# Receptance and key of the RWKV heads: two matmuls per k-tile in place of three

## The chip, the cores and the metric

The kernel runs on one core of one Trainium2 chip. Its time is the device time of one execution in microseconds; the number used for a kernel is the median of its runs. A lower time is better.

## The reference

A two-layer decoder trunk on 256 tokens of width 2048, in float32. Layer 0 mixes tokens with a short gated convolution, layer 1 with RWKV-7 time mixing; each is followed by a feed-forward part with a short convolution inside. All the change lies in layer 1, in two of its projections:

```python
xx = jnp.pad(x, ((0, 0), (1, 0), (0, 0)))[:, :-1] - x
xm = x[None] + xx[None] * mu[:, None, None, :]
xr, xw, xk, xv, xa, xg = xm[0], xm[1], xm[2], xm[3], xm[4], xm[5]
r = xr @ w_r
k = xk @ w_k
v = xv @ w_v
```

`r` is the receptance and `k` the key, each a 256 x 2048 by 2048 x 2048 product. They are then cut into 32 heads of 64 channels, and a recurrence over the tokens runs in every head.

## The kernel before

Precision: TensorE multiplies in a reduced float32 form, so each operand is kept as a high and a low part (`hl`, index 0 and 1), and a product is the sum of three matmuls: high by high, high by low, low by high. `mm3` (L144 to L147) issues these three. A weight arrives from memory as `raw` (1 MB, three buffers), and `split_w` makes its parts in pieces of 1024 columns: ScalarE writes the high part (L136), VectorE the low one (L137), into four rotating buffers `hl`.

Layer 0 and the ffn's up-projections use another form, `column` (L191 to L202): the activations' high and low part lie side by side for each k-tile, so one matmul of 512 columns gives high by high and high by low in the two halves of a PSUM bank, and a second one of 256 columns adds low by high to the second half. `column_sum` (L204 to L207) then copies one half out with ScalarE and adds the other with VectorE.

The heads: 16 pairs of heads are worked through in a software pipeline of four stages, written as Python generators (`rwkv_heads`, from L577). In one step, stage 3 of one pair, stage 2 of the next, stage 1 of the one after it and stage 0 of the newest take turns: each is advanced to its next `yield`, in the order 3, 2, 1, 0, until all are done. Stage 0 (L591) makes two small projections (`tw`, `ta`) and then receptance and key for 128 channels, 16 k-tiles each, from `wr[g]` and `wk[g]`, by `group_a`, which issues `mm3` 16 times on 256 columns and yields after every fourth k-tile. Both sums share one PSUM bank (tag "big", two buffers), key in the first half and receptance in the second; one ScalarE copy (L606) takes both out into `kr`. Stage 1 makes the chunk's decay and key terms from `kr` (a square at L635 that TensorE sums at L641, products at L666 and L670) and small matmuls of 64 x 64 blocks. Stage 2 inverts a 64 x 64 triangular matrix by levels (TensorE L724 and L734, VectorE L726, ScalarE L736, and a last step at L741 to L756). Stage 3 runs the recurrence over four chunks (L763 to L792) and the output's norm and gate.

Order: the code gives a priority; the framework's planner, which estimates when each instruction could start, writes the order of every engine's queue, so an instruction may be moved ahead of older ones that are not ready. TensorE's order in the trace shows this: a single matmul of a group of `mm3` can stand between pieces of other stages.

The activations: the shifted mixtures are made by `variant` (L484) for receptance (`xr`, L478), key (`xk`, in four tiles of `Early.tile`, L417) and the small projections (`lora`, L500). In the old layout a tile has the index order token block, k-tile, part, token: the high parts of the two token blocks of one k-tile lie apart, and an operand of 256 columns is two blocks of 128. The value projection reads the same tiles in blocks of 128 tokens, as weights (L438).

Of the kernel before, what the change touches and what calls it, by code (L numbers as in the profile page):

```python
# [11 lines left out]
F32 = mybir.dt.float32  # L12
F32R = mybir.dt.float32r
F16 = mybir.dt.float16
AF = mybir.ActivationFunctionType
ALU = mybir.AluOpType
# [65 lines left out]
def trunk(ctx: ExitStack, tc: tile.TileContext, x, ng, vec, cst, gnp, win, wout, up0, dn0, wl1, wv, wr, wk, wl2, wo,  # L82
# [108 lines left out]
    def column(src, xhl):  # L191


        ps = bank8(2, T)
        kt = 0
        for hl in load_w(src, 1024 if KT >= 8 else KT * P):
            for i in range(min(8, KT)):
                W = slice(i * P, (i + 1) * P)
                nc.tensor.matmul(ps, hl[:, 0, W], xhl[:, kt], start=kt == 0, stop=False)  # L199
                nc.tensor.matmul(ps[:, 1], hl[:, 1, W], xhl[:, kt, 0], start=False, stop=kt == KT - 1)  # L200
                kt += 1
        return ps[:, 0], ps[:, 1]  # L202

# [203 lines left out]
    class Early:  # L407
# [9 lines left out]
        def tile(self, q):  # L417
            t = self.pool.tile([P, NB, 4, 2, P], F32R, name=f"xkv{q}")
            return t, t.rearrange("p b k h c -> p (b k h c)").rearrange("p (h c) -> p h c", h=2)
# [14 lines left out]
        def mm(self, ps, hls, r, blk):  # L434
            for i in range(2 * len(hls)):
                kt = int(r * (RAWW // 512)) + i
                hl, c, xm = hls[i // 2], i % 2 * 512, self.xv[kt // 4]
                mm3(ps[blk], xm[:, blk, kt % 4, 0, :], xm[:, blk, kt % 4, 1, :], hl[:, 0, c:c + 512],  # L438
                    hl[:, 1, c:c + 512], kt == 0, kt == KT - 1)
# [7 lines left out]
        def mix(self, n):  # L447
# [7 lines left out]
            split(self.xv[n][:, 0, :, 0, :], self.xv[n][:, 0, :, 1, :], xm)  # L455
# [17 lines left out]
    def rwkv(xT, lhid, ctxv, early):  # L473
# [4 lines left out]
        xr = ctxv.enter_context(sbuf("rvr", 1, "right")).tile([P, NB, KT, 2, P], F32R, name="xr")  # L478
        xv = early.xv

        with tc.tile_pool(name="rvar", bufs=2, reuse_waits="tile") as vp:
            xx = vp.tile([P, NB, KT, P], F32, name="xx", bufs=1)

            def variant(m, k4, dst, blks=slice(0, NB), nk=4, whole=False):  # L484
                xm = vp.tile([P, NB, 4, P], F32, name="xm", bufs=3)[:, :, :nk]
                for i in range(nk):
                    kt = k4 + i
                    mu = vcol("mu", m * KT + kt)
                    if whole:
                        nc.vector.scalar_tensor_tensor(xm[:, blks, i], xx[:, blks, kt], mu, xT[:, blks, kt, 1:P + 1],  # L490
                                                       ALU.mult, ALU.add)
                    else:
                        nc.scalar.activation(xm[:, blks, i], xx[:, blks, kt], AF.Copy, scale=mu)
                if not whole:
                    nc.vector.tensor_tensor(out=xm[:, blks], in0=xm[:, blks], in1=xT[:, blks, k4:k4 + nk, 1:P + 1], op=ALU.add)
                split(dst[:, blks, :, 0, :], dst[:, blks, :, 1, :], xm[:, blks])
# [3 lines left out]
            def lora(which, ms):  # L500
                ps = [bank8(512) for _ in range(2)]
                kt = 0
                for r in range(KT * GC // RAWW):
                    for hl in load_w(wl1[which][:, r * RAWW:(r + 1) * RAWW], 1024):
                        for i in range(4):
                            if i % 2 == 0:
# [3 lines left out]
                                for m in dict.fromkeys(ms):  # L510
                                    vts[m] = xl[:, len(vts) * 1024:(len(vts) + 1) * 1024].rearrange(
                                        "p (b k h c) -> p b k h c", b=NB, k=2, h=2)
                                    variant(m, kt, vts[m], nk=2)
                            for j in range(2):
# [3 lines left out]
                                    vt[:, :, i % 2, 0, :], vt[:, :, i % 2, 1, :], kt == 0, kt == KT - 1)  # L518
# [32 lines left out]
            def variants():  # L551
                for k4 in range(0, KT, 4):
                    variant(0, k4, xr[:, :, k4:k4 + 4])
                    yield
# [22 lines left out]
    def rwkv_heads(scr, xk, xr, lhid, ctxv, fill):  # L577
# [4 lines left out]
        with tc.tile_pool(name="kz", bufs=1, reuse_waits="tile") as zp, tc.tile_pool(name="kx", bufs=2, reuse_waits="tile") as kx, \  # L582
# [8 lines left out]
            def stage0(g, st):  # L591
# [4 lines left out]
                for w, dst in ((0, st.tw), (1, st.ta)):  # L596
# [4 lines left out]
                ps = bank("big", 2, T)  # L601
                yield from group_a(wr[g], xsel(xr), ps[:, 1], 0)
                yield from group_a(wk[g], lambda kt, j: (xk[kt // 4][:, :, kt % 4, 0, :], xk[kt // 4][:, :, kt % 4, 1, :]),
                                   ps[:, 0], 0)
                st.kr = kx.tile([P, 2, T], F32, name="kr")
                nc.scalar.activation(st.kr, ps, AF.Copy)  # L606
# [539 lines left out]
```

## Time and profile before

| | us |
|---|---|
| median of 3 runs | 2588.75 |
| lowest and highest run | 2586.83 and 2589.52 |
| the profiled execution | 2590.17 |
| its span | 2588.4 |
| stage of the heads, by the first and last start of the copy L606 | 1269.2 to 1701.6 |

In the profile, PE is TensorE, PEld its weight loads, DVE is VectorE, ACT is ScalarE, POOL is GpSimd and SP the queue that issues most transfers. L145 is line 145 of the kernel. A row in order of time has the start in us, the duration in us, engine, line, operation, output and inputs by the program's names, their shape, a count, and in brackets how long the engine was idle before and what ended that. Matmuls are pipelined: the duration of one includes its way through the array, and the next one starts earlier.

### The profile page before, as it was taken

What the parts mean: (1) busy time and instruction counts of PE and PEld (TensorE: products, weight loads), DVE (VectorE), ACT (ScalarE), POOL (GpSimd) and SP (SyncE); (2) the same over time, 40 slices, a digit from 0 to 9 for tenths busy, and PEclk for the clock granted to TensorE, in tenths of its full rate; (3) what the DMA queues carried; (4) which work ended last, traced back from release to release, by engine and by line L of the source; (5) the groups of instructions that cost most, each with busy time, mean ns of one, the idle gap of its engine ahead of it and who ended that gap; (6) DMA issues with size and microseconds to landing.
All of it is one profiled execution on the core that took longest, in us unless ns stands there. A gap on an engine that the chain in (4) does not pass through costs nothing.

```text
span 2588.4 us, 44203 instructions
## 1 busy us (share of the span) xinstructions
PE 2545.5 (98%) x18284; PEld 2192.6 (85%) x18284; DVE 1689.0 (65%) x2419; ACT 1351.7 (52%) x2115; POOL 166.3 (6%) x239
## 2 busy tenths in 40 slices
PE   7999999999999999989999999999999999999998
PEld 7888888888888888878888888877888888888886
DVE  5666567777767655589756666665767767765555
ACT  5444456555555544469744444443655555554444
POOL 0000000000000000010222223220000000000000
PEclk9999999999999999999999999999999999999999
DMA  6555554555555555545523222335455555555553
GB/s 229 189 196 185 191 194 157 187 194 189 186 195 190 186 194 185 205 165 204 179 83 105 95 92 92 103 112 212 163 196 186 188 195 186 188 195 194 194 190 138
DMA packets 106986, 446.89 MB, mean 173 GB/s; under 512 B 29760, under 2 KB 47824, under 8 KB 57248
## 3 DMA queue, kind: packets, MB, share of 16 engines
q1 hardware_dynamic: 105328, 437.40, 48.6%
q0 software_dynamic: 1456, 6.66, 0.7%
q8 instruction: 143, 2.34, 0.4%
q14 instruction: 59, 0.48, 0.1%
HBM read 436.03 MB, written 8.00 MB: 172 GB/s over the span
## 4 chain that ended last, share of the span: by engine, by line
PE 93%; DVE 2%; ACT 2%; POOL 1%; issue 1%; DMA 1%; SPq 0%; DVEq 0%; POOLq 0%; ACTq 0%
PE tl L199 8%; PE big L199 8%; PE mn L199 8%; PE inv L199 8%; PE big L145 5%; PE big L146 5%; PE big L147 5%; PE tl L200 4%; PE big L200 4%; PE inv L200 4%; PE mn L200 4%; PE tl L145 3%; PE tl L147 3%; PE mn L145 3%; PE mn L147 3%; PE mn L146 2%
## 5 line engine op out<-in xcount | busy, mean ns | idle before, releaser
L137 DVE TENSOR_TENSOR hl<-raw,hl 128x1024 fp32r<-128x1024 f32 (+1 forms) x818 | 975.3, 1195 | 498.1 <-ACT hl L136 493.9
L136 ACT ACTIVATE hl<-raw 128x1024 fp32r<-128x1024 f32 (+1 forms) x818 | 841.8, 1031 | 568.4 <-PE big L147 150.8
L199 PE MATMUL tl<-xhl,hl 128*128 128x512 f32 x880 | 307.8, 391 | 0.0
L199 PE MATMUL big<-xhl,hl 128*128 128x512 f32 x880 | 307.8, 391 | 0.0
L199 PE MATMUL mn<-xhl,hl 128*128 128x512 f32 x864 | 302.2, 391 | 0.0
L199 PE MATMUL inv<-xhl,hl 128*128 128x512 f32 x864 | 301.9, 391 | 0.0
L200 PE MATMUL tl<-xhl,hl 128*128 128x256 f32 x880 | 246.2, 280 | 0.0
L200 PE MATMUL big<-xhl,hl 128*128 128x256 f32 x880 | 246.2, 280 | 0.0
L200 PE MATMUL mn<-xhl,hl 128*128 128x256 f32 x864 | 241.8, 280 | 0.0
L200 PE MATMUL inv<-xhl,hl 128*128 128x256 f32 x864 | 241.7, 280 | 0.0
L199 PEld LDWEIGHTS big<-xhl,hl 128*128 128x128 f32 x880 | 165.0, 187 | 36.2
L199 PEld LDWEIGHTS tl<-xhl,hl 128*128 128x128 f32 x880 | 165.0, 187 | 36.2
L199 PEld LDWEIGHTS inv<-xhl,hl 128*128 128x128 f32 x864 | 161.9, 187 | 35.7
L199 PEld LDWEIGHTS mn<-xhl,hl 128*128 128x128 f32 x864 | 161.9, 187 | 35.5
L200 PEld LDWEIGHTS tl<-xhl,hl 128*128 128x128 f32 x880 | 165.6, 188 | 0.0
L200 PEld LDWEIGHTS big<-xhl,hl 128*128 128x128 f32 x880 | 165.6, 188 | 0.0
L200 PEld LDWEIGHTS inv<-xhl,hl 128*128 128x128 f32 x864 | 162.6, 188 | 0.0
L200 PEld LDWEIGHTS mn<-xhl,hl 128*128 128x128 f32 x864 | 162.6, 188 | 0.0
L308 POOL TENSOR_TENSOR r<-s,nhalf 128x1 f32<-128x1 f32 x16 | 9.7, 606 | 1243.3 <-DVE s L306 1243.3
L145 PE MATMUL big<-xr,hl 128*128 128x256 f32 x268 | 82.8, 309 | 0.0
L145 PE MATMUL big<-xkv,hl 128*128 128x256 f32 x256 | 77.9, 304 | 0.0
L146 PE MATMUL big<-xr,hl 128*128 128x256 f32 x268 | 77.1, 288 | 0.0
(514 smaller groups left out, 4989.1 us busy)
## 6 DMA issues: line engine op xcount, KB each, us to landing
raw<-in_up_dram SPq DMA_DIRECT2D x172, 1024.0 KB, 4.8
raw<-in_dn_dram SPq DMA_DIRECT2D x88, 1024.0 KB, 4.8
raw<-in_win_dram SPq DMA_DIRECT2D x46, 1024.0 KB, 4.8
raw<-in_wout_dram SPq DMA_DIRECT2D x16, 1024.0 KB, 4.8
raw<-in_wv_dram SPq DMA_DIRECT2D x16, 1024.0 KB, 5.0
raw<-in_wr_dram SPq DMA_DIRECT2D x16, 1024.0 KB, 4.9
raw<-in_wk_dram SPq DMA_DIRECT2D x16, 1024.0 KB, 5.0
raw<-in_wo_dram SPq DMA_DIRECT2D x16, 1024.0 KB, 5.1
```

Of the source, the lines that this page charges most:

```text
L136: nc.scalar.activation(hl[:, 0, C], s[:, C], AF.Copy)
L137: nc.vector.tensor_tensor(out=hl[:, 1, C], in0=s[:, C], in1=hl[:, 0, C].bitcast(F32), op=ALU.subtract)
L145: nc.tensor.matmul(o, wh, xh, start=start, stop=False)
L146: nc.tensor.matmul(o, wh, xl, start=False, stop=False)
L147: nc.tensor.matmul(o, wl, xh, start=False, stop=stop)
L199: nc.tensor.matmul(ps, hl[:, 0, W], xhl[:, kt], start=kt == 0, stop=False)
L200: nc.tensor.matmul(ps[:, 1], hl[:, 1, W], xhl[:, kt, 0], start=False, stop=kt == KT - 1)
L308: nc.gpsimd.tensor_tensor(out=r, in0=s, in1=nhalf[:, 0:1], op=ALU.pow)
```

## The change

Receptance and key are computed in the form of `column`, with a new generator `column_a` that yields after every fourth k-tile as `group_a` does. For this the mixtures are laid out with the index order k-tile, part, token block, token, so that the 512 columns of one k-tile, high and low, are contiguous. All that writes or reads these tiles follows the new order. Each of the two projections has a PSUM bank of its own now (the same tag with two buffers); when its 16 k-tiles are done, ScalarE copies the second half into `kr` and VectorE adds the first half to it.

```diff
--- before.py
+++ after.py
@@ -200,6 +200,19 @@
                 nc.tensor.matmul(ps[:, 1], hl[:, 1, W], xhl[:, kt, 0], start=False, stop=kt == KT - 1)
                 kt += 1
         return ps[:, 0], ps[:, 1]
+
+    def column_a(src, x, ps):
+
+        kt = 0
+        for hl in load_w(src, 1024):
+            for i in range(8):
+                W = slice(i * P, (i + 1) * P)
+                xhl = x(kt).rearrange("p h b t -> p h (b t)")
+                nc.tensor.matmul(ps, hl[:, 0, W], xhl, start=kt == 0, stop=False)
+                nc.tensor.matmul(ps[:, 1], hl[:, 1, W], xhl[:, 0], start=False, stop=kt == KT - 1)
+                kt += 1
+                if kt % 4 == 0:
+                    yield
 
     def column_sum(dst, src, xhl):
         h, l = column(src, xhl)
@@ -415,8 +428,8 @@
             return [self.tile(q)[0] for q in range(KT // 4)]
 
         def tile(self, q):
-            t = self.pool.tile([P, NB, 4, 2, P], F32R, name=f"xkv{q}")
-            return t, t.rearrange("p b k h c -> p (b k h c)").rearrange("p (h c) -> p h c", h=2)
+            t = self.pool.tile([P, 4, 2, NB, P], F32R, name=f"xkv{q}")
+            return t, t.rearrange("p k h b c -> p (k h b c)").rearrange("p (h c) -> p h c", h=2)
 
         def pieces(self):
             q = itertools.count()
@@ -435,7 +448,7 @@
             for i in range(2 * len(hls)):
                 kt = int(r * (RAWW // 512)) + i
                 hl, c, xm = hls[i // 2], i % 2 * 512, self.xv[kt // 4]
-                mm3(ps[blk], xm[:, blk, kt % 4, 0, :], xm[:, blk, kt % 4, 1, :], hl[:, 0, c:c + 512],
+                mm3(ps[blk], xm[:, kt % 4, 0, blk, :], xm[:, kt % 4, 1, blk, :], hl[:, 0, c:c + 512],
                     hl[:, 1, c:c + 512], kt == 0, kt == KT - 1)
 
         def chunk(self, n):
@@ -452,7 +465,7 @@
             for i in range(4):
                 nc.vector.scalar_tensor_tensor(xm[:, i], xe[:, i], vcol("mu", mu + i), self.xT[:, 0, 4 * n + i, 1:P + 1],
                                                ALU.mult, ALU.add)
-            split(self.xv[n][:, 0, :, 0, :], self.xv[n][:, 0, :, 1, :], xm)
+            split(self.xv[n][:, :, 0, 0, :], self.xv[n][:, :, 1, 0, :], xm)
 
         def emit(self, blk):
             if blk == 0:
@@ -475,25 +488,26 @@
         scr = SimpleNamespace(
             v=dram.tile([T, D], F32, name="scr_v"),
             z=dram.tile([KT, P, T], F32, name="scr_z"))
-        xr = ctxv.enter_context(sbuf("rvr", 1, "right")).tile([P, NB, KT, 2, P], F32R, name="xr")
+        xr = ctxv.enter_context(sbuf("rvr", 1, "right")).tile([P, KT, 2, NB, P], F32R, name="xr")
         xv = early.xv
 
         with tc.tile_pool(name="rvar", bufs=2, reuse_waits="tile") as vp:
             xx = vp.tile([P, NB, KT, P], F32, name="xx", bufs=1)
 
             def variant(m, k4, dst, blks=slice(0, NB), nk=4, whole=False):
-                xm = vp.tile([P, NB, 4, P], F32, name="xm", bufs=3)[:, :, :nk]
+                xm = vp.tile([P, 4, NB, P], F32, name="xm", bufs=3)[:, :nk]
                 for i in range(nk):
                     kt = k4 + i
                     mu = vcol("mu", m * KT + kt)
                     if whole:
-                        nc.vector.scalar_tensor_tensor(xm[:, blks, i], xx[:, blks, kt], mu, xT[:, blks, kt, 1:P + 1],
+                        nc.vector.scalar_tensor_tensor(xm[:, i, blks], xx[:, blks, kt], mu, xT[:, blks, kt, 1:P + 1],
                                                        ALU.mult, ALU.add)
                     else:
-                        nc.scalar.activation(xm[:, blks, i], xx[:, blks, kt], AF.Copy, scale=mu)
+                        nc.scalar.activation(xm[:, i, blks], xx[:, blks, kt], AF.Copy, scale=mu)
                 if not whole:
-                    nc.vector.tensor_tensor(out=xm[:, blks], in0=xm[:, blks], in1=xT[:, blks, k4:k4 + nk, 1:P + 1], op=ALU.add)
-                split(dst[:, blks, :, 0, :], dst[:, blks, :, 1, :], xm[:, blks])
+                    nc.vector.tensor_tensor(out=xm[:, :, blks], in0=xm[:, :, blks],
+                                            in1=xT[:, blks, k4:k4 + nk, 1:P + 1].rearrange("p b k t -> p k b t"), op=ALU.add)
+                split(dst[:, :, 0, blks, :], dst[:, :, 1, blks, :], xm[:, :, blks])
 
             slots = itertools.cycle(((xpool, "xr0"), (xpool, "xr1"), (vp, "xl")))
 
@@ -509,13 +523,13 @@
                                 xl = pool.tile([P, XW], F32, name=name, bufs=1).bitcast(F32R)
                                 for m in dict.fromkeys(ms):
                                     vts[m] = xl[:, len(vts) * 1024:(len(vts) + 1) * 1024].rearrange(
-                                        "p (b k h c) -> p b k h c", b=NB, k=2, h=2)
+                                        "p (k h b c) -> p k h b c", b=NB, k=2, h=2)
                                     variant(m, kt, vts[m], nk=2)
                             for j in range(2):
                                 c = i * GC + j * P
                                 vt = vts[ms[j]]
                                 mm3(ps[j][:, :T].rearrange("p (b t) -> p b t", b=NB), hl[:, 0, c:c + P], hl[:, 1, c:c + P],
-                                    vt[:, :, i % 2, 0, :], vt[:, :, i % 2, 1, :], kt == 0, kt == KT - 1)
+                                    vt[:, i % 2, 0], vt[:, i % 2, 1], kt == 0, kt == KT - 1)
                             kt += 1
                         yield
                 hf = vp.tile([P, 2, T], F32, name="hf", bufs=1)
@@ -550,7 +564,7 @@
 
             def variants():
                 for k4 in range(0, KT, 4):
-                    variant(0, k4, xr[:, :, k4:k4 + 4])
+                    variant(0, k4, xr[:, k4:k4 + 4])
                     yield
 
             def shift(eng, k4, blks):
@@ -598,12 +612,12 @@
                         True, True)
                     nc.scalar.activation(dst, ps[:, w], AF.Tanh, scale=0.5, bias=hb[:, w, g:g + 1])
                 yield
-                ps = bank("big", 2, T)
-                yield from group_a(wr[g], xsel(xr), ps[:, 1], 0)
-                yield from group_a(wk[g], lambda kt, j: (xk[kt // 4][:, :, kt % 4, 0, :], xk[kt // 4][:, :, kt % 4, 1, :]),
-                                   ps[:, 0], 0)
                 st.kr = kx.tile([P, 2, T], F32, name="kr")
-                nc.scalar.activation(st.kr, ps, AF.Copy)
+                for i, w, x in ((1, wr, lambda kt: xr[:, kt]), (0, wk, lambda kt: xk[kt // 4][:, kt % 4])):
+                    ps = bank("big", 2, T)
+                    yield from column_a(w[g], x, ps)
+                    nc.scalar.activation(st.kr[:, i], ps[:, 1], AF.Copy)
+                    nc.vector.tensor_tensor(out=st.kr[:, i], in0=ps[:, 0], in1=st.kr[:, i], op=ALU.add)
                 yield
 
             hc = zp.tile([P, C_H], F32, name="hc")
```

## The prediction

> **What bounds the kernel now.** I read the page's engine shares first, then its chain of waits, then the busy time by stretch for the stage of the heads, then single instructions in order of time.
>
> ```profile
> span 2588.4 us, 44203 instructions
> ...
> PE 2545.5 (98%) x18284; PEld 2192.6 (85%) x18284; DVE 1689.0 (65%) x2419; ACT 1351.7 (52%) x2115; POOL 166.3 (6%) x239
> ...
> PE 93%; DVE 2%; ACT 2%; POOL 1%; issue 1%; DMA 1%; SPq 0%; DVEq 0%; POOLq 0%; ACTq 0%
> ```
>
> The first row has busy times, the second the chain that ended last: TensorE is both the busiest engine and 93% of the chain. The question is whether that holds in the stage that is edited. Busy time by stretch (busy us and instructions of each engine; then granted clock, DMA share, GB/s):
>
> ```profile
> 1262.00:1290.00 28.00, 26.06 (x277) 24.10 (x276) 16.54 (x28) 15.77 (x29) 8.02 (x10) 1.00 0.60 171
> 1290.00:1315.00 25.00, 22.65 (x308) 20.48 (x303) 12.95 (x21) 10.61 (x22) 6.22 (x7) 0.93 0.23 82
> 1340.00:1400.00 60.00, 59.95 (x915) 53.17 (x916) 40.02 (x83) 28.69 (x60) 16.62 (x22) 1.00 0.30 96
> 1400.00:1460.00 60.00, 59.95 (x918) 53.17 (x917) 40.05 (x84) 28.55 (x60) 16.57 (x22) 1.00 0.30 97
> ```
>
> It does: while the pairs run full, TensorE is busy 59.95 of 60 us, VectorE 40.0, ScalarE 28.6. Only the filling of the pipeline (the first two rows, 1262 to 1315) has TensorE idle, 4.3 us in all. What the change is worth in time is therefore what it takes off TensorE, as long as no new wait appears. Busy time does not tell that, since the modelled matmuls overlap (two of 0.28 us start 0.12 us apart, below); start-to-start distances do.
>
> **The cost of one k-tile as it is.** In the first pair nothing else runs, and its two projections stand in one row:
>
> ```profile
> 1256.85 0.28 PE L145 MATMUL big<-xr,hl 128*128 128x256 f32 x1
> ...
> 1263.74 0.28 PE L145 MATMUL tl<-lhid,hl 128*128 128x256 f32 x1
> ...
> 1263.97 0.28 PE L147 MATMUL tl<-lhid,hl 128*128 128x256 f32 x1
> ...
> 1268.60 0.28 PE L145 MATMUL big<-xr,hl 128*128 128x256 f32 x1
> ```
>
> Between the first and the last start lie 2 x 16 k-tiles x 3 = 96 matmuls, and three of the same size for the next pair's small projection: (1268.60 - 1256.85)/99 = 118.7 ns each, 356.1 ns a k-tile.
>
> **The cost after.** The new form, 512 columns and then 256, already runs in the mixer and the ffn:
>
> ```profile
> 500.26 0.39 PE L199 MATMUL tl<-xhl,hl 128*128 128x512 f32 x1
> 500.49 0.28 PE L200 MATMUL tl<-xhl,hl 128*128 128x256 f32 x1
> 500.61 0.39 PE L199 MATMUL tl<-xhl,hl 128*128 128x512 f32 x1
> ...
> 503.73 0.39 PE L199 MATMUL inv<-xhl,hl 128*128 128x512 f32 x1
> ```
>
> From 500.26 to 503.73 there are 10 k-tiles: 347 ns each. So the number of columns that stream, 768, is the same, and what goes is one matmul's fixed part: 356.1 - 347 = 9.1 ns a k-tile at best. The heads need not run at this stage's pace, though; just ahead of them 512-column matmuls of the value projection are slower:
>
> ```profile
> 1254.63 0.39 PE L146 MATMUL tl<-hl,xkv 128*128 128x512 f32 x1
> ...
> 1256.26 0.39 PE L147 MATMUL tl<-hl,xkv 128*128 128x512 f32 x1
> ```
>
> Seven distances in 1.63 us, 232.9 ns each. With that and the heads' own 118.7 a k-tile would take 351.6 ns, a gain of only 4.5 ns. I take 7 ns, between the two: the form is that of the first row, the place that of the second. There are 16 pairs x 2 projections x 16 k-tiles = 512 k-tiles, so the gain is 3.6 us, with 2.3 and 4.7 us as its ends.
>
> The Trainium skill has a rule that speaks against even this: in "TensorE: Matmul & The Clock Gate", section "Wait — 56ns, not 53.3ns?", a warm matmul is said to follow the one before by its columns at 2.4 GHz and a fixed 2.5 ns or so. By it the estimate would be 512 x 2.5 ns = 1.3 us of gain. The rows here do not agree with its distances (118.7 ns for 256 columns, where it gives 109), so the sum goes by the rows.
>
> **Where groups meet other work.** Both forms give way to the other stages after every fourth k-tile, so the number of planned groups stays at 128. A group in the running pipeline:
>
> ```profile
> 1303.93 1.07 PE L689 MATMUL tl<-BK,AR 64*64 64x128 f32 x16
> 1304.93 0.39 PE L145 MATMUL big<-xkv,hl 128*128 128x256 f32 x1
> 1305.15 0.28 PE L146 MATMUL big<-xkv,hl 128*128 128x256 f32 x1
> ...
> 1306.35 0.28 PE L147 MATMUL big<-xkv,hl 128*128 128x256 f32 x1
> 1306.57 0.31 PE L724 MATMUL inv<-WX,LT 64*64 64x64 f16 x8
> ```
>
> The first and the last distance are 0.22 us in place of 0.12: entering and leaving a run of full-width matmuls costs 0.10 us each, most likely weight loads that nothing covers. Changing the twelve matmuls to eight leaves these ends in place, so I cost them at nothing. But the planner also breaks up a group:
>
> ```profile
> 1317.77 0.29 PE L724 MATMUL inv<-WX,LT 64*64 64x64 f16 x8
> 1317.99 0.38 PE L147 MATMUL big<-xr,hl 128*128 128x256 f32 x1
> 1318.26 0.38 PE L145 MATMUL tl<-lhid,hl 128*128 128x256 f32 x1
> ```
>
> Here one matmul of a group stands alone as filler. With other instructions to place, it may break once more or once less in each step; that is 0.2 us x 16 = 3.2 us either way. I take zero, having no row that favours a side.
>
> **Taking the sums out of PSUM.** Rows of the old copy and of the two operations that replace it (min/median/max ns):
>
> ```profile
> L606 ACT ACTIVATE kr<-big x16: 575/597/598, 1269.2 to 1701.6; 128x512 f32<-128x512 f32 x16
> ...
> L206 ACT ACTIVATE s<-big x43: 367/385/386, 411.2 to 2327.9; 128x256 f32<-128x256 f32 x43
> ...
> L207 DVE TENSOR_TENSOR s<-big,s x43: 424/425/425, 411.6 to 2328.3; 128x256 f32<-128x256 f32 x43
> ```
>
> Per pair ScalarE does 2 x 0.385 in place of 0.597 us, VectorE 2 x 0.425 us more. The running stretches hold about two pairs per 60 us, so ScalarE goes to about 28.9 and VectorE to 41.7 of 60: neither becomes the bound. What counts is who stands behind them. Key's copy and its followers on ScalarE, with the TensorE instructions that need them:
>
> ```profile
> 1462.75 0.60 ACT L606 ACTIVATE kr<-big 128x512 f32<-128x512 f32 x1 [1.32 <-PE big L147]
> 1463.25 1.05 ACT L136 ACTIVATE hl<-raw 128x1024 fp32r<-128x1024 f32 x1
> 1464.19 0.59 ACT L736 ACTIVATE WX<-inv 128x512 f16<-128x512 f32 x1
> 1464.67 0.51 ACT L635 ACTIVATE sq<-kr,vecs 128x256 f32<-128x256 f32 x1
> ...
> 1464.84 0.30 PE L743 MATMUL inv<-WX,i16n 64*64 64x256 f16 x2
> ...
> 1465.42 0.61 PE L641 MATMUL tl<-csts,sq 128*128 128x2 f32 x4
> ```
>
> The square (L635) starts 1.92 us after the copy because a weight split and another copy stand between. The new copy and add end 0.81 us after 1462.75, so the square does not wait; the shorter copy lets WX end 0.2 us sooner, where L743 starts only 0.06 us behind it. Without that cover L641 would come up to 0.2 us late per pair, 3 us in all. I count no gain and no loss.
>
> Receptance's sum is new in the middle of a pair. It waits for the same matmul as a weight split does:
>
> ```profile
> 1303.55 1.06 ACT L136 ACTIVATE hl<-raw 128x1024 fp32r<-128x1024 f32 x1 [0.71 <-PE big L147]
> ...
> 1304.64 1.23 DVE L137 TENSOR_TENSOR hl<-raw,hl 128x1024 fp32r<-128x1024 f32 x1 [0.77 <-ACT hl L136]
> ...
> 1310.37 0.39 PE L145 MATMUL big<-xkv,hl 128*128 128x256 f32 x1
> ```
>
> The split waits until receptance's last matmul frees its buffer (1303.5), is complete at 1305.87, and its first user, key's ninth k-tile, comes at 1310.37: 4.5 us of cover for at most 0.81. Nothing is due from it. The second PSUM bank per pair was last read a whole pair earlier, so no matmul waits for it. The reordered activations are written by as many instructions of the same sizes; the value and small projections read blocks of the same sizes. No transfer is added or moved.
>
> **The sum.** The profiled execution took 2590.17 us (span 2588.4 and 1.8 around it), 1.4 above the median of 2588.75. 2590.17 - 3.6 = 2586.6 on its own scale, **2585.2 us** on that of the median. That is 0.14%; 0.2% (5.2 us, below 2583.6 or above 2593.9) is about what can be told from no change.
>
> **Rivals.**
>
> Fewer breaks: the planner has eight matmuls in place of twelve to use as filler and breaks once less per step. For it: the lone L147 above. Against: the gaps it fills are made by the same chains. 2585.2 - 3.2 = 2582.0 us, faster.
>
> More breaks: 2585.2 + 3.2 = 2588.4 us, no change; for and against as before, with the sign turned.
>
> Receptance's eviction in the way: ScalarE and VectorE take it ahead of the weight split, and key's matmuls wait for the split. For it: both are released by one matmul, and the eviction comes first in the code. It decides only once the 4.5 us of cover falls below 0.81 us; then each pair pays up to 0.81 us, 13 us, and the time is 2598 us, slower. Against: four weight buffers, and splits that the planner runs ahead of older code.
>
> The gain is not seen: the clock. In the row from 1290 to 1315 the granted clock is 0.93; 7% of 25 us is 1.7 us lost there. A second such stretch takes half of the gain: 2587 us.
>
> **How the numbers follow.** Forecast 0.43 (its own range 2584.0 to 2586.5), fewer breaks 0.32, more breaks 0.09, eviction in the way 0.09, a second stretch of low clock 0.07. The forecast's fast end lies near the 0.2% bound, so 0.05 of it counts as faster: faster 0.37, same 0.54 (0.38 + 0.09 + 0.07), slower 0.09. The range takes the larger gain with one break less per step (4.7 + 3.2, 2580.8) and the smaller with one more (2.3 + 3.2, 2589.7), and about a microsecond beyond each for the spread of the runs: 2580 to 2591. Left out are two breaks fewer and the eviction in the way.
>
> **What would show it.** In the first pair the distance from one 512-column start to the next should be 347 to 352 ns, and a group of four k-tiles in the running pipeline about 1.60 us in place of 1.64. TensorE should stay busy 59.9 of 60 us; the repeat of the pattern, 29.8 us now by the starts of L763 below, should fall by 0.15 to 0.3 us (32 k-tiles by 4.5 to 9.1 ns).
>
> ```profile
> 1407.93 1.02 PE mn L763 x16
> ...
> 1437.73 1.02 PE mn L763 x16
> ```
>
> It is wrong if that repeat does not fall, if TensorE waits for a weight split (L136, L137) at key's first or ninth k-tile, or if L641 or L743 gains an idle time.

## The result and the profile after

The changed kernel takes 2605.41 us (median of 6 runs, 2604.61 to 2607.36) beside 2589.14 us for the kernel before (6 runs, 2586.83 to 2589.58). The ratio is 1.0065, with a 95% interval of 1.0052 to 1.0078: slower by 0.65% or 16.3 us, where 3.6 us of gain were forecast. The time lies outside the predicted range.

The page after, its rows on the span, the busy times and the chain that ended last:

```profile
span 2602.8 us, 43199 instructions
PE 2549.5 (98%) x17772; PEld 2161.0 (83%) x17772; DVE 1699.8 (65%) x2451; ACT 1354.6 (52%) x2131; POOL 165.5 (6%) x239
PE 89%; ACT 3%; DVE 2%; POOL 2%; issue 1%; DMA 1%; SPq 0%; DVEq 0%; POOLq 0%; ACTq 0%
```

The 512 matmuls are gone (18284 to 17772). But TensorE holds 89% of the chain in place of 93%, and ScalarE and GpSimd have taken over 1% each. The loss is in the running pipeline. Busy time by stretch after, and the starts of the recurrence's first matmuls (L777 is L763 of before) in the chain in order of time:

```profile
1340.00:1400.00 60.00, 58.42 (x831) 47.14 (x830) 39.01 (x84) 28.02 (x57) 15.58 (x22) 1.00 0.29 95
1400.00:1460.00 60.00, 58.42 (x807) 47.02 (x806) 38.74 (x84) 27.24 (x57) 16.34 (x22) 1.00 0.28 95
```

```profile
1409.58 1.06 PE mn L777 x16
...
1440.76 1.06 PE mn L777 x16
```

TensorE now idles 1.58 of 60 us where it idled 0.05, at a full granted clock. One step of the pipeline takes 31.18 us in place of 29.80. About twelve such steps lie in the stage: 12 x 1.38 = 16.6 us, about the loss that the runs show.

What TensorE waits for is one ScalarE copy. From the waits between 1262 and 1760 us after (weight loads, then matmuls; us in total, times, longest):

```profile
PEld L768 <- ACT R L762: 14.9, 13, 1.5
PE inv L768 <- ACT R L762: 10.6, 13, 1.1
```

L762 is the copy that takes `R`, a late step of the triangular inverse, out of PSUM (L748 before). Why it is late stands in ScalarE's queue. First the kernel before, from key's copy on (that copy, L606, starts at 1462.75 and stands in the prediction), then the kernel after:

```profile
1464.19 0.59 ACT L736 ACTIVATE WX<-inv 128x512 f16<-128x512 f32 x1
1464.67 0.51 ACT L635 ACTIVATE sq<-kr,vecs 128x256 f32<-128x256 f32 x1
1465.07 0.51 ACT L646 ACTIVATE kk<-kr,vecs 128x256 f32<-128x256 f32 x1
1465.47 0.38 ACT L748 ACTIVATE R<-inv 128x256 f16<-128x256 f32 x1
1466.53 0.47 ACT L599 ACTIVATE tw<-tl,hb 128x256 f32<-128x256 f32 x1 [0.68 <-PE tl L147]
1466.90 0.38 ACT L756 ACTIVATE W<-inv 128x256 f32<-128x256 f32 x1
1468.27 0.42 ACT L654 ACTIVATE sq<-ri 128x256 f32<-128x256 f32 x1 [0.99 <-POOL ri L645]
```

```profile
1465.12 0.38 ACT L619 ACTIVATE kr<-big 128x256 f32<-128x256 f32 x1 [1.24 <-PE big L212]
1465.40 1.05 ACT L136 ACTIVATE hl<-raw 128x1024 fp32r<-128x1024 f32 x1
1466.35 0.50 ACT L649 ACTIVATE sq<-kr,vecs 128x256 f32<-128x256 f32 x1
1466.75 0.58 ACT L750 ACTIVATE WX<-inv 128x512 f16<-128x512 f32 x1
...
1468.01 0.47 ACT L613 ACTIVATE tw<-tl,hb 128x256 f32<-128x256 f32 x1 [0.28 <-PE tl L147]
1469.56 0.41 ACT L668 ACTIVATE sq<-ri 128x256 f32<-128x256 f32 x1 [1.08 <-POOL ri L659]
1469.88 0.37 ACT L762 ACTIVATE R<-inv 128x256 f16<-128x256 f32 x1
...
1471.45 0.38 ACT L770 ACTIVATE W<-inv 128x256 f32<-128x256 f32 x1
```

The same instructions stand there in another order. Before, `WX` came ahead of the square, and both `R` and `W` were out before the instruction that the queue has to wait for: `sq<-ri`, which spreads the norms `ri` over the channels (below: the spread) and needs GpSimd's power of them. After, the square is ahead of `WX`, and the spread is ahead of `R` and `W`. The spread waits in both kernels, 0.99 and 1.08 us; only after does it hold up what TensorE needs. Counted from the start of key's copy, `R` starts 2.72 us later before (1465.47 - 1462.75) and 4.76 us later after (1469.88 - 1465.12). GpSimd's power, and the matmul that needs `R` with the one ahead of it, in order of time after:

```profile
1468.50 1.03 POOL L659 TENSOR_TENSOR ri<-ri,nhalf 128x4 f32<-128x4 f32 x1
```

```profile
1469.12 0.40 PE L211 MATMUL big<-xr,hl 128*128 128x512 f32 x1
1470.30 0.31 PE L768 MATMUL inv<-WX,R 64*64 64x64 f16 x8 [0.79 <-ACT R L762]
```

So the chain of one step runs: square, sums on TensorE, power on GpSimd (ends 1469.53), spread on ScalarE, `R`, and then TensorE, idle for 0.79 us. Other matmuls cover part of the 2.04 us by which `R` is later. The 0.79 us are not the whole of the 1.38 us by which a step is longer. They count from the modelled end of the matmul before; by the starts the gap is 1.18 us, where a matmul of 512 columns takes 0.23. And the planner breaks up more groups around it: the runs of receptance's and key's matmuls with nothing between them number 10 in a step before and 12 after. At the 0.2 us that the prediction puts on a break, that is an estimate of 0.4 us. Where the remainder lies was not taken apart.

The matmuls themselves did what the change says. In order of time after, the first pair's receptance and one group in the running pipeline; then a group of the same length where the 512-column matmul is cut in two (the experiment `three`, below):

```profile
1255.12 0.40 PE L211 MATMUL big<-xr,hl 128*128 128x512 f32 x1
...
1260.69 0.39 PE L211 MATMUL big<-xkv,hl 128*128 128x512 f32 x1
...
1479.80 0.50 PE L211 MATMUL big<-xr,hl 128*128 128x512 f32 x1
...
1481.38 0.34 PE L799 MATMUL mn<-SV,xr 128*64 128x64 f32 x4
```

```profile
1484.07 0.39 PE L211 MATMUL big<-xr,hl 128*128 128x256 f32 x1
...
1485.68 0.83 PE L807 MATMUL mn<-SV,xr 64*64 64x64 f32 x16
```

Sixteen k-tiles in 5.57 us are 348 ns each, where 347 to 352 were foreseen. The group takes 1.58 us against 1.61 with three matmuls, but other matmuls follow the two. Over all unbroken groups that start and end between 1320 and 1690 us, the mean is 1.572 us after (72 groups) and 1.598 before (86) and in `three` (72): 0.026 us x 128 groups = 3.3 us of gain.

### The profile page after: what moved, and what is told of

It reads as the page before. It is cut to its first block, busy times and chain, and to the rows that moved or that the text cites. A ratio compares the mean times of both kernels' runs of the same rounds, so it can differ in the third digit from the quotient of the medians.

```text
span 2602.8 us, 43199 instructions
## 1 busy us (share of the span) xinstructions
PE 2549.5 (98%) x17772; PEld 2161.0 (83%) x17772; DVE 1699.8 (65%) x2451; ACT 1354.6 (52%) x2131; POOL 165.5 (6%) x239
## 4 chain that ended last, share of the span: by engine, by line
PE 89%; ACT 3%; DVE 2%; POOL 2%; issue 1%; DMA 1%; SPq 0%; DVEq 0%; POOLq 0%; ACTq 0%
PE big L199 8%; PE tl L199 8%; PE mn L199 8%; PE inv L199 8%; PE big L211 4%; PE tl L200 4%; PE big L200 4%; PE inv L200 4%; PE mn L200 4%; PE mn L145 2%; PE mn L147 2%; PE mn L146 2%; PE tl L145 2%; PE tl L147 2%; PE big L145 2%; PE inv L147 2%
## 5 line engine op out<-in xcount | busy, mean ns | idle before, releaser
L211 PE MATMUL big<-xr,hl 128*128 128x512 f32 x256 | 100.3, 417 | 0.0
L211 PE MATMUL big<-xkv,hl 128*128 128x512 f32 x256 | 97.9, 417 | 0.0
L212 PE MATMUL big<-xr,hl 128*128 128x256 f32 x256 | 76.1, 297 | 0.0
```

Of the source, the lines that this page charges most:

```text
L211: nc.tensor.matmul(ps, hl[:, 0, W], xhl, start=kt == 0, stop=False)
L212: nc.tensor.matmul(ps[:, 1], hl[:, 1, W], xhl[:, 0], start=False, stop=kt == KT - 1)
```

## The experiments

Theory A: the new matmul form costs the time, by its own pace or because the planner has fewer pieces to fill gaps with. Theory B: the new layout of the activations does. Theory C: the separate evictions turn the planned order of ScalarE's queue, and the wait for GpSimd then stands ahead of what TensorE needs. Each experiment was timed beside the kernel before on its chip (medians 2588.91 to 2589.63), and the ratios below are against that; a "step" is the repeat of the recurrence's first matmuls near 1400 to 1470 us.

### Which part: the layout alone, and three matmuls again

`lay` keeps the changed layout and takes back the rest: the old matmuls, one bank, one copy.

```diff
-                for i, w, x in ((1, wr, lambda kt: xr[:, kt]), (0, wk, lambda kt: xk[kt // 4][:, kt % 4])):
-                    ps = bank("big", 2, T)
-                    yield from column_a(w[g], x, ps)
-                    nc.scalar.activation(st.kr[:, i], ps[:, 1], AF.Copy)
-                    nc.vector.tensor_tensor(out=st.kr[:, i], in0=ps[:, 0], in1=st.kr[:, i], op=ALU.add)
+                ps = bank("big", 2, T)
+                yield from group_a(wr[g], lambda kt, j: (xr[:, kt, 0], xr[:, kt, 1]), ps[:, 1], 0)
+                yield from group_a(wk[g], lambda kt, j: (xk[kt // 4][:, kt % 4, 0], xk[kt // 4][:, kt % 4, 1]), ps[:, 0], 0)
+                nc.scalar.activation(st.kr, ps, AF.Copy)
```

> The new layout of the activations alone, with the old three matmuls, the one PSUM bank and the one copy of receptance and key together. If the order that the planner writes for ScalarE is the cause, 2589 us (within 2 of before): the planned order of ScalarE and TensorE is that of before. If the layout costs (slower writes of the mixtures or slower reads by TensorE), up to 2605 us. A step of the pipeline should repeat after 29.8 us in the first case, 31.2 us in the second.

Measured: 2589.46 us, ratio 0.9998 (0.9989 to 1.0007), step 29.82 us. The layout costs nothing: theory B falls.

`three` is the changed kernel with its 512-column matmul cut into two of 256.

```diff
-                nc.tensor.matmul(ps, hl[:, 0, W], xhl, start=kt == 0, stop=False)
+                nc.tensor.matmul(ps[:, 0], hl[:, 0, W], xhl[:, 0], start=kt == 0, stop=False)
+                nc.tensor.matmul(ps[:, 1], hl[:, 0, W], xhl[:, 1], start=False, stop=False)
```

> The changed kernel with its 512-column matmul cut back into two of 256, into the two halves of the bank: new layout, new banks and new copy and add, old number of matmuls. Planned order of ScalarE: square before WX, and R behind the spread of the norms, as in the changed kernel. If that order is the cause: 2605 us plus the 3 us of the extra matmuls, 2606 to 2609, with the wait of L768's successor for R of some 0.8 us a step. If the form of the matmuls is the cause: 2589 us.

Measured: 2608.46 us, ratio 1.0072 (1.0057 to 1.0087), step 31.62 us. With as many matmuls as before, and at the old pace, the time is not back; it is 3 us higher. Theory A falls, and what is left is the evictions and what they do to the order.

### The order on ScalarE

`order3` is the changed kernel with three edges that only fix an order on ScalarE: the square and `kk` behind the newest `WX` copy in the code, the spread behind the newest `R` copy. Nothing waits for another engine because of them.

```diff
+            last = {}
+
+            def after_last(name):
+                return tc.issue_after(last[name].ins) if name in last else nullcontext()
...
-                nc.scalar.activation(sq, kr, AF.Square, scale=vcol("kk", g))
+                with after_last("WX"):
+                    nc.scalar.activation(sq, kr, AF.Square, scale=vcol("kk", g))
...
-                nc.scalar.activation(kk, kr, AF.Identity, scale=vcol("kk", g))
+                with after_last("WX"):
+                    nc.scalar.activation(kk, kr, AF.Identity, scale=vcol("kk", g))
...
-                nc.scalar.activation(rx, ri.unsqueeze(2).broadcast_to([P, 4, 64]), AF.Copy)
+                with after_last("R"):
+                    nc.scalar.activation(rx, ri.unsqueeze(2).broadcast_to([P, 4, 64]), AF.Copy)
...
-                    nc.scalar.activation(WX, ps, AF.Copy)
+                    last["WX"] = nc.scalar.activation(WX, ps, AF.Copy)
...
-                nc.scalar.activation(R16, ps, AF.Copy)
+                last["R"] = nc.scalar.activation(R16, ps, AF.Copy)
```

> The changed kernel with three issue-order edges on ScalarE (no waits): a pair's square and scaled key behind the older pair's last WX, the spread of the norms behind the older pair's R. ScalarE's planned order at the start of a step is then that of before. If the order is the cause: 2585 us (2583 to 2588), a step of 29.6 us and no wait of TensorE for R. If the added VectorE operations or the matmul form are the cause: 2600 us or more.

Measured: 2581.52 us, ratio 0.9969 (0.9957 to 0.9982), 24 us faster than the changed kernel, 8.1 us faster than the one before, and 1.5 us below the range that I expected. ScalarE's queue, the busy time of a stretch and the steps in the chain of this kernel:

```profile
1459.69 0.38 ACT L770 ACTIVATE R<-inv 128x256 f16<-128x256 f32 x1
1460.74 0.47 ACT L618 ACTIVATE tw<-tl,hb 128x256 f32<-128x256 f32 x1 [0.68 <-PE tl L147]
1461.11 0.38 ACT L778 ACTIVATE W<-inv 128x256 f32<-128x256 f32 x1
1462.48 0.41 ACT L676 ACTIVATE sq<-ri 128x256 f32<-128x256 f32 x1 [0.99 <-POOL ri L665]
```

```profile
1340.00:1400.00 60.00, 60.00 (x875) 49.30 (x869) 41.59 (x89) 29.87 (x62) 16.82 (x23) 1.00 0.30 96
```

```profile
1402.90 1.02 PE mn L785 x16
...
1432.34 1.02 PE mn L785 x16
```

`R` and `W` are ahead of the spread again (`W` without an edge of its own). The spread waits as long as it did (0.99 us); TensorE has no idle time, and a step takes 29.44 us. This is what theory C says.

`keyfirst` turns the two projections around, so that receptance's eviction, not key's, comes at the end.

```diff
-                for i, w, x in ((1, wr, lambda kt: xr[:, kt]), (0, wk, lambda kt: xk[kt // 4][:, kt % 4])):
+                for i, w, x in ((0, wk, lambda kt: xk[kt // 4][:, kt % 4]), (1, wr, lambda kt: xr[:, kt])):
```

> The changed kernel with key ahead of receptance, nothing else. Key's sum is then complete half a pair earlier, so the square can run before the step's start and does not stand ahead of WX. If the order is the cause: 2582 to 2588 us, a step of at most 29.7 us. If the column form or the extra eviction costs by itself: 2600 us or more.

Measured: 2589.47 us, ratio 1.0000 (0.9991 to 1.0009), step 29.57 us: the step is as expected, the time outside both ranges. The step is a quarter of a microsecond better than before, but the filling of the pipeline is worse: the same stretch of busy time, in this kernel and then in `order3`, shows the granted clock (the number behind GpSimd's count) at 0.88 and 1.00.

```profile
1262.00:1290.00 28.00, 23.30 (x167) 19.03 (x165) 14.05 (x25) 13.57 (x26) 10.35 (x17) 0.88 0.55 154
```

```profile
1262.00:1290.00 28.00, 26.17 (x241) 21.88 (x239) 19.56 (x34) 17.55 (x35) 9.06 (x10) 1.00 0.62 184
```

There 3.4 us go to the clock and TensorE idles 2.9 us more (23.30 against 26.17 busy). The first recurrence starts at 1320.45 us, 5.8 us later than in `order3` (1314.67) and 1.8 later than in the kernel before (1318.69), and that eats most of the 3 us that twelve steps of 0.25 us gain. Whether it holds in every run is not shown. `W` still stands behind a waiting spread here (0.61 us), and TensorE waits for it 0.45 us a step.

### Which edge, and how much each is worth

`order5` keeps only the edge that puts the spread behind `R`; `order4` keeps only the one that puts the square behind `WX`. First the edit of `order5`:

```diff
                nc.scalar.activation(sq, kr, AF.Square, scale=vcol("kk", g))
...
                nc.scalar.activation(kk, kr, AF.Identity, scale=vcol("kk", g))
...
-                nc.scalar.activation(rx, ri.unsqueeze(2).broadcast_to([P, 4, 64]), AF.Copy)
+                with after_last("R"):
+                    nc.scalar.activation(rx, ri.unsqueeze(2).broadcast_to([P, 4, 64]), AF.Copy)
```

> The changed kernel with one of the three edges only: the spread of the norms (the copy of ri) behind the older pair's R on ScalarE. The square still stands ahead of WX. If R's place behind the spread is most of the loss, the wait of TensorE for R of 0.8 to 1.1 us a step goes: 2605 - 13 x 0.8 to 1.1 = 2591 to 2595 us. If it is rather the square ahead of WX, which makes all that follows late: 2600 us or more.

Measured: 2591.87 us, ratio 1.0014 (1.0004 to 1.0024), step 30.14 us. TensorE's wait for `R` is gone, and one for `W` has taken its place: `W` is still behind the spread. From this kernel's waits, same columns as above:

```profile
PE mn L783 <- ACT W L776: 5.8, 12, 0.5
```

And `order4`:

```diff
-                nc.scalar.activation(sq, kr, AF.Square, scale=vcol("kk", g))
+                with after_last("WX"):
+                    nc.scalar.activation(sq, kr, AF.Square, scale=vcol("kk", g))
...
                nc.scalar.activation(kk, kr, AF.Identity, scale=vcol("kk", g))
...
                nc.scalar.activation(rx, ri.unsqueeze(2).broadcast_to([P, 4, 64]), AF.Copy)
```

> The changed kernel with the other edge only: the square behind the older pair's last WX. The planner then also places R ahead of the spread; the scaled key still stands ahead of WX. If the square's place is the root: 2582 to 2588 us. If the whole old order is needed: 2590 us or more.

Measured: 2633.44 us, ratio 1.0178 (1.0152 to 1.0204), the slowest kernel of the study. The first case is out, and a loss of this size I had not seen coming. The planner now put `R` ahead of the spread but left `W` behind it, and the spread comes to its place early. In order of time, this kernel's spread and `W` on ScalarE and the waiting matmul on TensorE in an earlier step; then the row of that wait, and the busy time up to just behind this idle time, in the 6.8 us that follow, in a later step, and in the whole running stage:

```profile
1458.60 0.42 ACT L674 ACTIVATE sq<-ri 128x256 f32<-128x256 f32 x1 [2.41 <-POOL ri L665]
1458.92 0.36 ACT L776 ACTIVATE W<-inv 128x256 f32<-128x256 f32 x1
```

```profile
1350.98 1.24 PE L783 MATMUL mn<-xr,W 64*64 64x128 f32 x16 [1.54 <-ACT W L776]
```

```profile
PE mn L783 <- ACT W L776: 18.4, 12, 1.5
```

```profile
1340.00:1351.80 11.80, 10.26 (x165) 8.33 (x164) 6.75 (x12) 6.47 (x15) 4.86 (x6) 1.00 0.09 29
1351.80:1358.60 6.80, 6.80 (x59) 5.58 (x56) 2.28 (x3) 2.02 (x3) 0.00 (x0) 0.50 0.25 70
1492.60:1524.30 31.70, 30.17 (x425) 24.37 (x425) 20.49 (x43) 14.31 (x31) 8.57 (x11) 1.00 0.29 91
1340.00:1702.00 362.00, 345.13 (x4550) 278.88 (x4550) 218.89 (x459) 153.95 (x322) 91.45 (x117) 0.93 0.26 84
```

ScalarE stands for 2.41 us with `W` behind the spread, TensorE idles for 1.54 us, and right behind that idle time its clock is at 0.50 for 6.8 us. Not every step has that: TensorE idles as long before 1492.60, and the clock stays at 1.00. Over the whole running stage the clock is 0.93: 7% of 362 us, 25 us, go to the clock. A step with a full clock takes 31.70 us (1492.60 to 1524.30, from one idle time to the next), 1.9 us more than in the kernel before, and twelve of them make 23 us. Together that is 48 us, which is what the profiled execution (2637.26 us) takes more than the kernel before (2589.28); the median is 44 us above it, with runs from 2628.58 to 2643.76.

`order7` adds to `order4` that the spread stays behind `W`; `order6` has that edge alone.

```diff
-                nc.scalar.activation(rx, ri.unsqueeze(2).broadcast_to([P, 4, 64]), AF.Copy)
+                with after_last("W"):
+                    nc.scalar.activation(rx, ri.unsqueeze(2).broadcast_to([P, 4, 64]), AF.Copy)
...
-                nc.scalar.activation(st.W32, ps, AF.Copy, scale=1.0 / NRES)
+                last["W"] = nc.scalar.activation(st.W32, ps, AF.Copy, scale=1.0 / NRES)
```

> The kernel of the square's edge alone (2633 us) with one edge more: the spread of the norms behind the older pair's W. There TensorE waited 1.5 to 1.9 us a step for W, which stood behind the spread on ScalarE. If that wait, and the low clock after it, is all of the loss: 2581 to 2586 us. If the scaled key ahead of WX is what costs: 2600 us or more.

Measured for `order7`: 2588.18 us, ratio 0.9996 (0.9987 to 1.0005), step 29.73 us. That is 2 us above the range of the first case and far from the second. One edge takes away 45 us: `order4`'s time was the spread ahead of `W`, the lost clock with it. The scaled key still stands ahead of `WX`.

> The changed kernel with a single edge: the spread behind the older pair's W (and so behind its R). The square stays ahead of WX. If only what waits behind the spread costs: 2582 to 2588 us, a step of 29.4 to 29.8 us. If the square's place costs too: as with the spread behind R alone, 2590 to 2594 us.

Measured for `order6`: 2586.68 us, ratio 0.9994 (0.9984 to 1.0003), step 29.59 us, with the square still ahead of `WX`. So the steps fall from 31.18 us (changed kernel) to 30.14 (`R` ahead of the spread), 29.59 (`W` too) and 29.44 (`order3`, the square and the scaled key behind `WX` as well). The first two steps down, 1.04 and 0.55 us, come with taking `R` and then `W` out from behind the spread, which waits 1.08 us in the changed kernel, 0.68 in `order5` and not at all in `order6`. How much of the 0.55 is `W`'s wait alone is open: in `keyfirst`, with much the same wait for `W` as in `order5`, a step takes 29.57 us. The place of the square makes some 0.15 us a step either way: `order3` is shorter than `order6`, `order7` longer.

### No edge at all: the spread on GpSimd

`rxpool` leaves the planner free and takes the waiting instruction off ScalarE; GpSimd, busy for 6% of the span, spreads the norms itself.

```diff
-                nc.scalar.activation(rx, ri.unsqueeze(2).broadcast_to([P, 4, 64]), AF.Copy)
+                nc.gpsimd.tensor_copy(rx, ri.unsqueeze(2).broadcast_to([P, 4, 64]))
```

> The changed kernel with the spread of the norms done by GpSimd, which makes the norms, in place of ScalarE; no edges. The square stays ahead of WX, but nothing in ScalarE's queue waits for GpSimd any more. If that wait, with R behind it, is the loss: 2583 to 2590 us, and no wait of TensorE for R or W over 0.5 us a step. If the square's place ahead of WX is the loss by itself: 2600 us or more.

Measured: 2586.63 us, ratio 0.9992 (0.9982 to 1.0001), step 29.59 us, the same as `order6`, with no wait of TensorE for `R` and 0.3 us a step for `W` (weight loads). Here no order is prescribed and the square is still ahead of `WX`; only the wait in ScalarE's queue is gone. That shows the cause without the edges.

### Where the gain over the kernel before comes from

`order3_three` is `order3` with the 512-column matmul cut in two, as in `three`.

```diff
-                nc.tensor.matmul(ps, hl[:, 0, W], xhl, start=kt == 0, stop=False)
+                nc.tensor.matmul(ps[:, 0], hl[:, 0, W], xhl[:, 0], start=kt == 0, stop=False)
+                nc.tensor.matmul(ps[:, 1], hl[:, 0, W], xhl[:, 1], start=False, stop=False)
```

> The kernel with the three edges (2581.5 us), with the 512-column matmul cut into two of 256: what is left is the price of the matmul form in the good order. 512 k-tiles by 4.5 to 9.1 ns: 2.3 to 4.7 us more, 2584 to 2586 us. If the form is worth more where TensorE does not wait: 2589 us or more.

Measured: 2584.07 us, ratio 0.9982 (0.9973 to 0.9992), step 29.60 us. Each against the kernel before on its own chip, `order3` gains 8.1 us and this one 5.2: the matmul form is worth 2.9 us in the good order. In the bad order it is 2.6 us (18.9 lost by `three`, 16.3 by the changed kernel). By the intervals the two differences carry some 4 and 5 us of uncertainty, so neither is clear of zero by itself; that they agree with each other and with the groups' 3.3 us is what speaks for them.

`before_ord` is the kernel before with the three edges of `order3`, of which one is shown.

```diff
-                nc.scalar.activation(rx, ri.unsqueeze(2).broadcast_to([P, 4, 64]), AF.Copy)
+                with after_last("R"):
+                    nc.scalar.activation(rx, ri.unsqueeze(2).broadcast_to([P, 4, 64]), AF.Copy)
```

> The kernel before with the same three edges. Its planned order meets them in the running pipeline, so if the edges only restore the old order, 2589 us (within 2 of before). If they improve the order beyond what it was (the filling of the pipeline, say), 2583 to 2586 us, and that part of the gain of the changed kernel with edges is not the matmuls'.

Measured: 2590.66 us, ratio 1.0006 (0.9996 to 1.0015), step 29.82 us. The kernel before already had this order, and the edges give it nothing. What `order3_three` gains, 5.2 us, therefore comes from the separate evictions, with the banks and additions that go with them.

`halves` tests that on the kernel before: the one copy of 512 columns becomes two of 256, key's half first, and nothing else is changed.

```diff
-                nc.scalar.activation(st.kr, ps, AF.Copy)
+                nc.scalar.activation(st.kr[:, 0], ps[:, 0], AF.Copy)
+                nc.scalar.activation(st.kr[:, 1], ps[:, 1], AF.Copy)
```

> The kernel before, with its one copy of key and receptance cut into two (key's half, then receptance's): old layout, old matmuls, one bank, no VectorE operation added. Key is there some 0.2 us sooner, and the planner puts the square and the scaled key ahead of WX, and the spread ahead of W (behind R). If an early key by itself turns the order, and the order is the loss: 2600 to 2635 us, with a wait of TensorE for W. If the loss needs the column form, its banks or its additions: 2588 to 2591 us.

Measured: 2583.00 us, ratio 0.9977 (0.9968 to 0.9986), step 29.48 us: faster, which I had expected of neither theory. Its queue on ScalarE from receptance's copy (the last of the two) on, in order of time:

```profile
1455.70 0.38 ACT L607 ACTIVATE kr<-big 128x256 f32<-128x256 f32 x1
1455.97 0.51 ACT L636 ACTIVATE sq<-kr,vecs 128x256 f32<-128x256 f32 x1
...
1456.77 0.59 ACT L737 ACTIVATE WX<-inv 128x512 f16<-128x512 f32 x1
...
1458.36 0.38 ACT L749 ACTIVATE R<-inv 128x256 f16<-128x256 f32 x1
...
1459.17 0.42 ACT L655 ACTIVATE sq<-ri 128x256 f32<-128x256 f32 x1
1459.49 0.37 ACT L757 ACTIVATE W<-inv 128x256 f32<-128x256 f32 x1
```

The order turns here too: the square is ahead of `WX`, and the spread is ahead of `W`. But the square starts 0.27 us behind the start of the last copy (in the changed kernel a weight split of 1.05 us stands between the two), so the norms are ready when ScalarE comes to the spread; it has no wait, and `W` follows at once. This narrows the theory. This order by itself is not what costs; it costs when the instruction at the head of the queue stands waiting with TensorE's copies behind it. The run also shows that a shorter copy ahead of key's followers is enough to turn the planned order, without the new matmuls.

## Why the prediction was wrong, point by point

**The bound.** Right. TensorE set the end, and the time went up as TensorE began to wait: idle for 1.58 us in 60 where it had 0.05.

**The cost of a k-tile.** Right in size. I took 7 ns a k-tile and 3.6 us, with 2.3 and 4.7 us as ends; the groups give 3.3 us, and the two pairs of runs with and without the form 2.9 and 2.6. The Trainium skill's rule that I set beside it ("TensorE: Matmul & The Clock Gate", section "Wait — 56ns, not 53.3ns?", a fixed 2.5 ns a matmul) gave an estimate of 1.3 us; all three readings are above that, though the uncertainty of the runs alone would not rule it out.

**Where groups meet other work.** The ends of a group kept their cost (1.572 us for an unbroken group in the mean, 1.60 foreseen). The breaks were put at zero, and that did not hold: the changed kernel has 12 runs of these matmuls in a step where the kernel before has 10, two more breaks, in the direction of "More breaks". They belong to the turned order and not to having fewer matmuls to place: `three`, with the old number of matmuls and that order, has 12 as well, while `order3`, `order6` and `rxpool` are back at 10.

**Taking the sums out of PSUM.** This is the step that failed, and its sentence is "I count no gain and no loss". The durations were right, as the grouped rows after show (min/median/max ns):

```profile
L619 ACT ACTIVATE kr<-big x32: 359/383/385, 1261.6 to 1714.6; 128x256 f32<-128x256 f32 x32
L620 DVE TENSOR_TENSOR kr<-big,kr x32: 413/424/425, 1262.0 to 1715.0; 128x256 f32<-128x256 f32 x32
```

What failed was that I left ScalarE's followers in the order that the trace of before showed, and only moved their times: `WX` 0.2 us sooner, the square no later. But the order is the planner's to write anew after any edit, and it placed the square ahead of `WX`, and the spread ahead of `R` and `W`. `WX` started 1.63 us behind key's copy where it had 1.44, so it was 0.2 us later, not sooner. And my rows of that queue ended with the square, two instructions ahead of `R`: the spread, with 0.99 us of waiting for GpSimd already in the trace of before, has no place in the prediction. It could be read there as a wait that was free only because nothing urgent stood behind it. With it priced at about 1 us a step, a turned order would have been a rival at 12 x 1 = 12 us slower; the change made it 16.3.

**The rival on the other side.** "Receptance's eviction in the way" had the engine and the sign, and a price of 13 us, but another mechanism: matmuls of the two projections wait for a split's VectorE part 0.7 us in all before and not at all after (1262 to 1760 us), and the prolonged wait is the one for `R`. What would show it listed the repeat of the pattern, which rose by 1.38 us instead of falling by 0.15 to 0.3, and named the wrong waits beside it.

**Where the gain went.** It is there in the matmuls, and is overpaid by the turned order: 16.3 us lost against the kernel before, 24 us against the same kernel in the good order. Of the 8.1 us that `order3` gains, 2.9 are the matmul form. The other 5.2 are the separate evictions, which were worth nothing in my sum; 12 steps of 0.22 us (29.82 to 29.60) make 2.6 of them. Where the rest arises is not shown: in the profiles of `order3_three` and of the kernel before the first recurrence starts at the same time (1318.70 and 1318.69), and both have a stretch of clock 0.93 in the filling, but the profiled execution of `order3_three` is the slowest of its ten runs.

**What stays open.** Why the planner turns the order: its estimates are in no trace. `halves` shows that a shorter copy for key is enough to turn it. There key is out 0.22 us sooner (0.38 us after the copy's start, 0.60 before). In the changed kernel it is not: VectorE's addition (1465.53, 0.42 us) ends 0.83 us after the copy's start. So a key that is ready sooner is not the reason there, unless the planner's estimates say otherwise. Why `halves` gains 0.34 us a step, when TensorE was busy 59.95 of 60 us before, is not settled either, nor is the part of a step's 1.38 us that the idle time and the breaks leave. The fastest kernel of the study is `order3`, the change with its order held: 2581.52 us, 0.31% below the kernel before.

## What to carry to other kernels

Where a planner writes the queues, a trace shows one order, not the order: cutting one copy of 0.60 us into two of 0.38 can turn it (`halves`). So price what stands at the head of an in-order queue and waits for a slow engine: its wait is free only as long as nothing that the bounding engine needs is planned behind it. Hold such an order with an edge, or move the waiting instruction to the engine that it waits for.

## What the runs showed of the hardware

In `order4`, TensorE has an idle time of 1.53 or 1.54 us in each of twelve steps. Behind seven of them the granted clock fell to 0.50, for 3.4 us (two times), 6.8 us (four) or 17 us (one); behind the other five it stayed at 1.00, and so it did behind an idle time of 2.47 us in the filling of the same kernel (up to 1298.46; clock 1.00 from 1290 to 1315). Idle times of 0.79 us a step left it at 1.00 (the changed kernel, 1340 to 1460 us). The Trainium skill ("TensorE: Matmul & The Clock Gate", section "Why this matters for your kernels") puts the idle time to be avoided at about 3 us; this trace agrees only in part, since the clock fell behind seven idle times of half that length. What decides between the seven and the five, and whether the small matmuls that follow the idle time have a part in it, is not shown.

A power of 128 x 4 numbers holds GpSimd for 1.03 us, longer than ScalarE's copy of 128 x 512 took (0.60 us).
